# Wider weight chunks for the raw experts: 2048 and 1536 columns in place of 1024, 1024, 1024 and 512

## The chip, the cores and the metric

The kernel runs as one program on one core of a Trainium2 chip (one NeuronCore: TensorE, VectorE, ScalarE, GpSimd, SyncE and 16 DMA engines). The metric is device microseconds (us) of one execution, the median of several runs. A difference of less than 0.2% between two such medians is not told apart here.

## The reference, cut to what matters

Two layers over 256 latent tokens and 256 context tokens of width 1024, all in float32. Layer 0 is a token-mixing MLP and a dense SwiGLU. Layer 1 is windowed attention and a mixture of eight SwiGLU experts, of which each of the 256 latent tokens uses two. The change lies in the experts alone:

```
D_MODEL = 1024; D_FF = 3584; N_EXPERTS = 8; TOP_K = 2
logits = (xt @ w_router).astype(jnp.float32)          # xt: 256 x 1024
top_v, top_i = lax.top_k(logits, TOP_K)
gates = sum(one_hot(top_i) * softmax(top_v))
for e in range(N_EXPERTS):
    y = y + gates[:, e:e + 1] * ((silu(xt @ w_gate[e]) * (xt @ w_up[e])) @ w_down[e])
```

Each expert has three float32 matrices of 3.67 million elements, 44 MB in all; eight experts are 352 MB that are read once.

## The kernel before, in words

Everything ahead of the experts (the first layer, attention, the router) is not touched. The experts begin at about 816 us of the span and last to its end.

**Slots and modes.** The experts are worked off in eight slots, `MODES = "SLSMMSMS"`. Slot 0 is expert 0; the others are given to experts by how many tokens they got. The mode says how many token rows a slot holds: S has 64 rows (one tile of 64), M has 96 rows (three tiles of 32), L has 128. L splits its weights into two halves of fewer bits and multiplies three times; S and M ("raw") feed the float32 weights straight to TensorE as the moving operand, with the tokens as the stationary one. Since an S tile has 64 columns of tokens, two column strips of the array (M: four) work on different columns of the weight row, and their results stand in different partitions of one PSUM bank (`columns`, L1512).

**Chunks and units.** `CH = (1024, 1024, 1024, 512)` cuts the 3584 hidden columns. `expert_units` (L1095) lists the loads in order: for a chunk the gate matrix, then the up matrix, in units of 1 MB, then the down rows of the chunk before. A unit of a 1024-column chunk is 256 weight rows, two in each partition, each a piece of 4 KB in memory; one of the 512-column chunk has four pieces of 2 KB; a unit of down has two whole rows that lie together, 8 KB (in M's last chunk two pieces of 4 KB). An expert is 42 units: 24 + 4 of gate and up, 14 of down.

**Buffers.** Each unit goes into a buffer of 8 KB per partition. After the first 21 the buffers are taken in the fixed order of `CYCLE` (18 names; `yh` and `side1` drop out early, so that 16 are left for the raw experts). All loads are issued by SyncE (SP), in the order of the units; a load waits until the last reader of its buffer is done, and the loads behind it wait too.

**Order on TensorE.** `chunk` (L1692) writes TensorE's order out by hand: gate units of chunk j, up units of chunk j, then the down units of the chunk before. In between stand the transposes of the hidden rows (`transposed_rows`, L1574), and one small step per unit from the list `extras`: the gather of the next expert's tokens (`gather_raw`, L1431: 16 matmuls for each expert), the matrix that brings results back (`back_raw`), and the scatter of an expert's result to token rows (`scattered`, L1625), in which the 64 rows of half a tile are the contraction and both halves use different row strips of the array.

**The end.** After the last down unit come `scaled` (L1615), the last scatter, the final norm and the output.

Of the kernel before, what the change touches and what calls it, by code (L numbers as in the profile page):

```python
# [59 lines left out]
ORDER = ('xgb0', 'xgb1', 'wsx', 'wst5', 'hc', 'wst2', 'wst4', 'yh')  # L60
# [17 lines left out]
MODES = "SLSMMSMS"  # L78
PARTS = {"S": (64, 1), "M": (32, 3)}
# [52 lines left out]
def body(tc, nc, I, out, dbg=None):  # L132
# [9 lines left out]
    with top:  # L142
# [151 lines left out]
        hx = [ph.tile([P, 4, 256], F32, name=f"hx{i}", bufs=1) for i in range(2)]  # L294
# [772 lines left out]
        CH = (1024, 1024, 1024, 512)  # L1067
        ids = {}

        class Expert:  # L1070
# [14 lines left out]
            def long(self, w):  # L1085
                return self.mode != "M" or w == 1024
# [8 lines left out]
        def expert_units(exs):  # L1095
            last = None
            for ex in exs:
                c0 = 0
                for w in CH:
                    k = 2 * 1024 // w  # L1100
                    for which in ("gate", "up"):
                        for r0 in range(0, D, k * P):
                            yield ex, (which, r0, k, c0, w), (k, w)
                    if last is not None:
                        yield from down_units(*last)
                    last = ex, c0, w
                    c0 += w
# [6 lines left out]
        SIZES = {"xgb": 2 * UNIT, "sg": UNIT // 2}  # L1114

        def fill_halves(tiles, src, shape):
            k, n = shape
            return [fill(t, src[:, k // 2 * i:k // 2 * (i + 1)], (k // 2, n)) for i, t in enumerate(tiles)]
# [17 lines left out]
        loaded = [fill_halves([early["sg"], early["at"][:, :UNIT // 2]], *source(first_units[0]))]  # L1136
        loaded += [in_halves(fill(early[n], *source(u))) for n, u in zip(ORDER, first_units[1:])]
# [24 lines left out]
        def stage_load(n, u, behind_):  # L1162
            src, shape = source(u)
            with tc.issue_after(last_early) if behind_ else ExitStack():
                if n == "hx":
                    return fill_halves(early["hx"], src, shape)
                if n in early:
                    return in_halves(fill(early[n], src, shape))
                p = {"wst": wst, "wst3": cur.get("wst3"), "wd": mp}[n]
                return in_halves(fill(p.tile([P, UNIT], F32, name=n, bufs=BUFS[n]), src, shape))  # L1170

        class Halves:
# [5 lines left out]
            def half(self):  # L1178
                if self.raw is None:
                    u = self.units.pop(0)  # L1180
                    self.raw = [moe_load(u), u[2], u[0].mode]
                v, (k, n), mode = self.raw
# [3 lines left out]
                if mode != "L":  # L1186
                    self.ready.append(src)
                    return
# [18 lines left out]
        def raw_row(u, k):  # L1207
            m = u[0].shape[1]
            return u[k // m][:, k % m, :]
# [7 lines left out]
        wrg = con.tile([P, DT, NE], F32, name="wrg")  # L1217
        wrb = con.tile([P, 2, NE], F32, name="wrb")
        ws = s2t()[:, :DT * NE].rearrange("p (k e) -> p k e", k=DT)
        V.tensor_mul(ws, wr, modT[1][:, 24:32, 0:1].to_broadcast([P, DT, NE]))  # L1220
        V.tensor_mul(wrg, wr, G[1][1][:, :, 0:1].to_broadcast([P, DT, NE]))
# [46 lines left out]
        early["hx"] = [ph.tile([P, UNIT // 2], F32, name=f"hx{i}", bufs=1) for i in range(2)]  # L1268
        fills = FILLS.split()
        split_unit = source(units[len(loaded) + [n for n in fills if n != "hx0"].index("hx1")])  # L1270
        parts = []
        for n in fills:
            if n[:2] == "hx":
                src, (k, n_) = split_unit
                i = int(n[2])
                with tc.issue_after(last_early):
                    parts.append(fill(early["hx"][i], src[:, k // 2 * i:k // 2 * (i + 1)], (k // 2, n_)))
                if i:
                    loaded.append(parts)
# [96 lines left out]

        def gather(ex, first=False):
            if ex.mode != "L":
                yield from gather_raw(ex, first)
# [38 lines left out]
        def gather_raw(ex, first):  # L1418
            n = SLOTCAP[ex.col]
            oh = s2t()[:, :2 * n].rearrange("p (c s) -> p c s", c=2)  # L1420
            one_hot(oh, ex, 2, n)
            for _ in range(GY):
                yield
            ex.tile = ph.tile([P, UNIT], F32, name="w", bufs=4)
            ex.xg = ex.tile[:, :DT * n].rearrange("p (d s) -> p d s", d=DT)
            for d0 in range(0, DT, 4):
                ps = tp_ps()
                for d in range(d0, d0 + 4):
# [5 lines left out]
                scaled_rows(ex, ps, d0, 4, n, first)  # L1434
# [3 lines left out]
        def back_raw(ex):  # L1438
# [10 lines left out]
            ex.oht = ex.tile[:, UNIT - 256 * k:].rearrange("p (k t) -> p k t", k=k)  # L1449
# [6 lines left out]
        def scaled_rows(ex, ps, d0, k, n, first):  # L1456
            for d in range(k):
                dst, src, g, b = ex.xg[:, d0 + d, :], ps[:, d * n:(d + 1) * n], G[1][1][:, d0 + d, 0:1], mod(1, 3, d0 + d, 0)
# [52 lines left out]

        def columns(place, xs, wrow, n, start, stop):  # L1512
# [6 lines left out]
        def gate_up(ex, w, steps=()):  # L1519
            per = 2 * 1024 // w  # L1520
# [8 lines left out]
            for k0 in range(0, DT, per):  # L1529
# [15 lines left out]
        def transposed_rows(ex, w):  # L1545
# [7 lines left out]

            if ex.mode == "L":
                at = RB["at"].rearrange("p i (f s) -> p i f s", s=P)
# [9 lines left out]
            nb = w * n // P // P  # L1565
            size = D * n // P
            blocks = [(t, f) for t in range(k) for f in range(nb)]
            at = {}

            def some_blocks(bs):  # L1570
                pt = tp_ps()
                dst = s2t()[:, :len(bs) * P]
                for i, (t, f) in enumerate(bs):
                    PE.transpose(pt[:, i * P:i * P + P], block_of(size * t, f), ident)  # L1574
                    at[t, f] = dst[:, i * P:i * P + P].rearrange("p (h s) -> p h s", s=n)
                A.copy(dst, pt[:, :len(bs) * P])  # L1576

            return [lambda b=b: some_blocks(blocks[b:b + 4]) for b in range(0, len(blocks), 4)], at

        def down(ex, j, w, at):  # L1580
            nf = w // P
            raw = ex.mode != "L"
            if raw:
                n, nt = PARTS[ex.mode]
                nb = nf * n // P
# [207 lines left out]
```

## Time and profile before

| what | value |
|---|---|
| time, median of 3 runs (lowest to highest) | 1680.15 us (1679.33 to 1680.38) |
| the profiled execution's own time | 1678.95 us |
| its span, first to last instruction | 1676.9 us |
| TensorE busy | 1638.3 us, 98% |
| VectorE, ScalarE, GpSimd busy | 47%, 28%, 2% |
| TensorE clock granted, mean | 0.993 |
| bytes moved by the kernel's own queue | 475.73 MB, 75.7% of 16 engines' span |

The profiled execution took 1678.95 us from outside and 1676.9 us from its first to its last instruction, so 2.05 us lie around the span. A matmul of float32 operands shows as two records, so the counts of records are twice those of the program. The ends of matmuls are modelled, so that the duration of a group runs a little into the next; the price of a unit is best read from the start of one group to the start of the next. "Issue" is idle time in which an engine waited for nothing that the profile shows.

### The profile page before, as it was taken

What the parts mean: (1) busy time and instruction counts of PE and PEld (TensorE: products, weight loads), DVE (VectorE), ACT (ScalarE), POOL (GpSimd) and SP (SyncE); (2) the same over time, 40 slices, a digit from 0 to 9 for tenths busy, and PEclk for the clock granted to TensorE, in tenths of its full rate; (3) what the DMA queues carried; (4) which work ended last, traced back from release to release, by engine and by line L of the source; (5) the groups of instructions that cost most, each with busy time, mean ns of one, the idle gap of its engine ahead of it and who ended that gap; (6) DMA issues with size and microseconds to landing.
All of it is one profiled execution on the core that took longest, in us unless ns stands there. A gap on an engine that the chain in (4) does not pass through costs nothing.

```text
span 1676.9 us, 31753 instructions
## 1 busy us (share of the span) xinstructions
PE 1638.3 (98%) x13501; PEld 1122.9 (67%) x13501; DVE 780.9 (47%) x1540; ACT 475.7 (28%) x910; POOL 37.3 (2%) x33
## 2 busy tenths in 40 slices
PE   7999999999999999999999999999999999999997
PEld 4678988888887878888536785355665653556532
DVE  5579678777677856896306984001001001010011
ACT  4434542222222223675215772100000101001001
POOL 0000000000000000032000000000000000000000
PEclk9999999999999999999999999999999999999999
DMA  9865335444455532316999999999999999999994
GB/s 310 284 216 188 125 126 201 151 158 153 142 175 177 191 135 101 101 64 226 392 385 411 412 381 355 408 410 411 407 409 407 383 384 408 409 411 406 405 407 174
DMA packets 178996, 477.83 MB, mean 285 GB/s; under 512 B 9080, under 2 KB 64544, under 8 KB 165152
## 3 DMA queue, kind: packets, MB, share of 16 engines
q1 hardware_dynamic: 178848, 475.73, 75.7%
q8 instruction: 108, 1.77, 0.4%
q14 instruction: 40, 0.33, 0.1%
HBM read 474.65 MB, written 1.05 MB: 284 GB/s over the span
## 4 chain that ended last, share of the span: by engine, by line
PE 93%; DVE 2%; DMA 2%; issue 1%; ACT 1%; SPq 1%; POOL 0%; DVEq 0%; ACTq 0%
PE mm L1516 38%; PE mm L232 15%; PE mm L233 15%; PE mm L234 15%; PE tp L1431 2%; PE tp L1625 1%; PE tp L1574 1%; DMA wst<-in_ada_w_dram 1%; PE mm L1025 1%; DMA side<-in_ctx_dram 1%; PE tp L1010 1%; PE mm L459 1%; PE tp L1446 0%; PE mm L430 0%; DMA side<-in_x_dram 0%
## 5 line engine op out<-in xcount | busy, mean ns | idle before, releaser
L1707 DVE TENSOR_TENSOR sg<-sg,mm 128x512 f32<-128x512 f32 (+2 forms) x47 | 25.6, 569 | 492.3 <-PE mm L1516 489.8
L232 PE MATMUL mm<-b,w 128*128 128x512 f32 (+1 forms) x560 | 206.3, 369 | 0.0
L233 PE MATMUL mm<-b,w 128*128 128x512 f32 (+1 forms) x560 | 205.0, 366 | 0.0
L234 PE MATMUL mm<-b,w 128*128 128x512 f32 (+1 forms) x560 | 204.7, 366 | 0.0
L1516 PE MATMUL mm<-wst,w 128*32 128x256 f32 (+3 forms) x2528 | 195.8, 393 | 4.8 <-issue 4.8
L168 ACT CAST w<-wst 128x512 fp32r<-128x512 f32 (+1 forms) x186 | 112.1, 653 | 170.3 <-PE mm L233 128.4
L496 DVE SCALAR_TENSOR_TENSOR s<-wst,cT,s 128x512 f32<-128x512 f32 x224 | 153.2, 745 | 11.5 <-DMA wst<-in_ada_w_dram 11.5
L1516 PEld LDWEIGHTS mm<-wst,w 128*32 128x32 f32 (+1 forms) x2528 | 96.6, 117 | 90.9 <-issue 53.6
L169 DVE TENSOR_TENSOR w<-wst,w 128x512 fp32r<-128x512 f32 (+1 forms) x186 | 127.1, 725 | 64.2 <-ACT w L168 63.7
L1576 ACT COPY s<-tp 128x512 f32<-128x512 f32 (+2 forms) x37 | 18.6, 503 | 380.8 <-PE tp L1574 321.6
L232 PEld LDWEIGHTS mm<-b,w 128*128 128x128 f32 x560 | 105.6, 189 | 19.6 <-issue 2.5
L234 PEld LDWEIGHTS mm<-b,w 128*128 128x128 f32 x560 | 105.6, 189 | 17.1
L233 PEld LDWEIGHTS mm<-b,w 128*128 128x128 f32 x560 | 105.7, 189 | 16.6 <-DVE b L169 0.2
L1516 PE MATMUL mm<-wst,s 128*32 128x256 f32 (+1 forms) x1104 | 96.3, 417 | 0.1
L232 PE MATMUL mm<-b,side 128*128 128x512 f32 (+1 forms) x240 | 91.0, 379 | 0.0
L234 PE MATMUL mm<-b,side 128*128 128x512 f32 (+1 forms) x240 | 90.0, 375 | 0.0
L233 PE MATMUL mm<-b,side 128*128 128x512 f32 (+1 forms) x240 | 90.0, 375 | 0.0
L1516 PEld LDWEIGHTS mm<-wst,s 128*32 128x32 f32 (+1 forms) x1104 | 44.2, 115 | 47.0 <-issue 27.9
L232 PE MATMUL mm<-w,b 128*128 128x512 f32 (+1 forms) x192 | 73.5, 384 | 0.0
L233 PE MATMUL mm<-w,b 128*128 128x512 f32 (+1 forms) x192 | 72.4, 378 | 0.2 <-DVE w L169 0.2
L234 PE MATMUL mm<-w,b 128*128 128x512 f32 (+1 forms) x192 | 72.1, 376 | 0.0
L1516 PE MATMUL mm<-wd,w 128*32 128x256 f32 (+2 forms) x864 | 70.6, 404 | 0.0
(399 smaller groups left out, 2586.6 us busy)
## 6 DMA issues: line engine op xcount, KB each, us to landing
wst<-in_moe_w_down_dram SPq DMA_DIRECT2D x51, 1024.0 KB, 14.0
wst<-in_moe_w_up_dram SPq DMA_DIRECT2D x50, 1024.0 KB, 15.6
wst<-in_moe_w_gate_dram SPq DMA_DIRECT2D x48, 1024.0 KB, 13.5
wst<-in_ada_w_dram SPq DMA_DIRECT2D x40, 1024.0 KB, 5.2
wd<-in_moe_w_up_dram SPq DMA_DIRECT2D x18, 1024.0 KB, 13.9
xgb<-in_moe_w_gate_dram SPq DMA_DIRECT2D x16, 1024.0 KB, 14.9
wd<-in_moe_w_down_dram SPq DMA_DIRECT2D x16, 1024.0 KB, 14.8
xgb<-in_moe_w_down_dram SPq DMA_DIRECT2D x15, 1024.0 KB, 16.4
```

The lines of the kernel that those rows point to most:

```text
L168: A.copy(hi, src)
L169: V.tensor_sub(lo, src, hi)
L232: PE.matmul(ps, sh, mh, start=start, stop=False)
L233: PE.matmul(ps, sh, ml, start=False, stop=False)
L234: cur["pe"] = PE.matmul(ps, sl, mh, start=False, stop=stop).ins
L459: PE.matmul(ps[j:j + 32, 256 * w:256 * w + 256], ones[:, :32], acc_[s][:, 256 * half_:256 * half_ + 256], start=True, stop=True)
L496: V.scalar_tensor_tensor(acc_[s], u[:, k, :], c_, acc_[s], op0=OP.mult, op1=OP.add)
L1010: PE.transpose(pt[:, kc * P:kc * P + P], pp[b][h4][:, kc * P:kc * P + P], ident)
L1431: PE.matmul(ps[:, (d - d0) * n:(d - d0 + 1) * n], acct[c, h][:, i * P:(i + 1) * P], oh[:, c, :], start=(c == 0), stop=(c == 1))
L1516: PE.matmul(ps[n * g:n * g + n, c0:c0 + w], x, wrow[:, w * g:w * g + w], start=start and first, stop=stop and last)
L1576: A.copy(dst, pt[:, :len(bs) * P])
L1707: V.tensor_mul(x, x, p)
```

## The change

For S and M slots the hidden columns are cut into two chunks, 2048 and 1536; L keeps its four. A unit of gate or up is then one weight row per partition: 8 KB (1 MB in all) in the first chunk, 6 KB (768 KB, in a buffer that could hold 1 MB) in the second. An expert has 46 units: 16 of 1 MB and 16 of 768 KB of gate and up, and 14 of down. The down rows of M's last chunk (now six units) are still pieces of 4 KB.

The rest makes room for it. A chunk of M fills three PSUM banks with 512 (384) columns each, one per tile, and one of S two banks. The hidden rows `sg` and their transposes `at` get one buffer each. The scatter of M works by its 32-row tiles (`scattered`, `quarters`). Two neighbouring slots share one gather (`GROUPED`), 160 token columns wide. The loads that were kept in halves are whole, and the router's scaled weights reuse a tile.

```diff
+GROUPED = (2, 3), (4, 5), (6, 7)
...
-ORDER = ('xgb0', 'xgb1', 'wsx', 'wst5', 'hc', 'wst2', 'wst4', 'yh')
+ORDER = ('at', 'xgb0', 'xgb1', 'wsx', 'wst5', 'hc', 'wst2', 'wst4', 'yh')
...
-        CH = (1024, 1024, 1024, 512)
+        CH = {"L": (1024, 1024, 1024, 512), "S": (2048, 1536), "M": (2048, 1536)}
...
-                return self.mode != "M" or w == 1024
+                return self.mode != "M" or w == 2048
...
-                for w in CH:
-                    k = 2 * 1024 // w
+                for w in CH[ex.mode]:
+                    k = max(2 * 1024 // w, 1)
...
+        def group(ex):
+            for g in GROUPED:
+                if ex.e is None and ex.col in g:
+                    return [order[s] for s in g]
+            return [ex]
...
+        def subs(ex, w):
+            if ex.mode == "S":
+                return [(c, min(1024, w - c)) for c in range(0, w, 1024)]
+            return [(0, w)]
+
+        def pieces(ex, w):
+            n, k = PARTS[ex.mode]
+            return [(t, c, v, v * n // P) for c, v in subs(ex, w) for t in range(k)]
...
-                place, ps = raw_banks(ex, w)
                 n, nt = PARTS[ex.mode]
+                parts = pieces(ex, w)
+                banks = [mm_ps() for _ in parts]
+                ps = [b[:, :hw] for b, (_, _, _, hw) in zip(banks, parts)]
...
-                        columns(place, [ex.xg[:, k, n * t:n * t + n] for t in range(nt)], raw_row(u, k - k0), n, start, stop)
+                        r = raw_row(u, k - k0)
+                        for b, (t, c, v, _) in zip(banks, parts):
+                            columns([(b, 0, True, True)], [ex.xg[:, k, n * t:n * t + n]], r[:, c:c + v], n, start, stop)
...
         def scattered(ps, ex, ys, c):
+            n = PARTS[ex.mode][0]
+            per = 512 * P // (D * n)
             for i, y in enumerate(ys):
-                for h in range(2):
-                    hs = slice(64 * h, 64 * h + 64)
-                    PE.matmul(ps[h], ex.oht[hs, i, c * P:(c + 1) * P], y[hs, :], start=(i == 0), stop=(i == len(ys) - 1))
+                for q in range(P // n):
+                    hs = slice(n * q, n * q + n)
+                    c0 = c % per * y.shape[-1]
+                    PE.matmul(ps[q][:, c0:c0 + y.shape[-1]], ex.oht[hs, i, c * P:(c + 1) * P], y[hs, :],
+                              start=(i == 0 and c0 == 0), stop=(i == len(ys) - 1 and c % per == per - 1))
+
+        def quarters(ex, y):
+            ps = [tp_ps() if q % 2 else mm_ps() for q in range(4)]
+            for c in range(2):
+                scattered(ps, ex, y, c)
+                yield
...
-                    if j == 2 and i + 1 < len(exs):
+                    if j == (2 if ex.mode == "L" else 1) and i + 1 < len(exs) and exs[i + 1] is group(exs[i + 1])[0]:
                         extras.append(gather(exs[i + 1]))
```

**On SP, the loads of slot 0.** The first rows are before, the second after; a name ahead of the arrow is the buffer, and behind the tensor stands the shape in the buffer, partitions first.

```order
L179 DMA yh<-in_moe_w_gate_dram 128x2x1024
L179 DMA wst<-in_moe_w_gate_dram 128x2x1024 x2
L179 DMA hx_7078<-in_moe_w_down_dram 128x1024
L179 DMA wst<-in_moe_w_gate_dram 128x2x1024
L179 DMA wd<-in_moe_w_up_dram 128x2x1024 x3
L179 DMA side<-in_moe_w_up_dram 128x2x1024
L179 DMA w<-in_moe_w_down_dram 128x2048 x2
L179 DMA wst_7096<-in_moe_w_down_dram 128x2048
```

```order
L180 DMA wst_6715<-in_moe_w_gate_dram 128x2048
L180 DMA wst_6713<-in_moe_w_gate_dram 128x2048
L180 DMA wst_6714<-in_moe_w_gate_dram 128x2048
L180 DMA yh<-in_moe_w_up_dram 128x2048
L180 DMA wst<-in_moe_w_up_dram 128x2048 x2
L1123 DMA hx<-in_moe_w_gate_dram 128x768
L180 DMA wst<-in_moe_w_up_dram 128x2048
L180 DMA wd<-in_moe_w_up_dram 128x2048 x3
L180 DMA side<-in_moe_w_up_dram 128x2048
L180 DMA w<-in_moe_w_gate_dram 128x1536 x2
L180 DMA wst_7091<-in_moe_w_gate_dram 128x1536
```

Each load of two rows of 1024 columns has become one row of 2048; the loads that follow are gate rows of 1536 columns, where down rows of the first chunk stood.

**On TensorE, the second half of the last M slot (slot 6).** Before, these are the last gate and up units of its 512-column chunk, with the transposes (L1574) of the chunk before; after, the first gate units of its 1536-column chunk, with transposes (L1605) and the scatter of slot 5 (L1662).

```order
L1574 MATMUL tp<-cst,sg 128x128 x4
L1516 MATMUL mm<-wsx,w 32x128 x48
L1574 MATMUL tp<-cst,sg 128x128 x2
L1516 MATMUL mm<-wst_6716,w 32x128 x48
L1516 MATMUL mm<-hc,w 32x128 x48
L1516 MATMUL mm<-wst_6714,w 32x128 x48
L1516 MATMUL mm<-wst_6715,s_12787 32x256 x8
```

```order
L1605 MATMUL tp<-cst,sg 128x128 x4
L1540 MATMUL mm<-wst,w 32x384 x12
L1605 MATMUL tp<-cst,sg 128x128 x4
L1540 MATMUL mm<-wd,w 32x384 x12
L1605 MATMUL tp<-cst,sg 128x128 x4
L1662 MATMUL tp<-s_11255,w 128x512
L1662 MATMUL mm<-s_11255,w 128x512
L1540 MATMUL mm<-wd,w 32x384 x24
L1662 MATMUL tp<-s_11255,w 128x512
L1662 MATMUL mm<-s_11255,w 128x512
L1540 MATMUL mm<-side,w 32x384 x12
```

A 1 MB unit of the narrow chunk was 48 matmuls of 128 columns; there is no such unit any more, and a 768 KB unit is 12 matmuls of 384 columns.

**On TensorE, the scatter of slot 3 (M) to one half of the tokens.** The first rows are before (three tiles by two halves of 64 rows, 512 columns), the second after (the second and the third tile, each by four quarters of 32 rows, 256 columns; the first tile stands ahead of them in the same way).

```order
L1625 MATMUL tp_10478<-s2_10406,w_8723 128x512
L1625 MATMUL mm_10479<-s2_10406,w_8723 128x512
L1625 MATMUL tp_10478<-s2_10407,w_8723 128x512
L1625 MATMUL mm_10479<-s2_10407,w_8723 128x512
L1625 MATMUL tp_10478<-s2_10408,w_8723 128x512
L1625 MATMUL mm_10479<-s2_10408,w_8723 128x512
```

```order
L1662 MATMUL mm_10044<-s2_9992,w_8105 128x256
L1662 MATMUL tp_10045<-s2_9992,w_8105 128x256
L1662 MATMUL mm_10046<-s2_9992,w_8105 128x256
L1662 MATMUL tp_10047<-s2_9992,w_8105 128x256
L1662 MATMUL mm_10044<-s2_9993,w_8105 128x256
L1662 MATMUL tp_10045<-s2_9993,w_8105 128x256
L1662 MATMUL mm_10046<-s2_9993,w_8105 128x256
L1662 MATMUL tp_10047<-s2_9993,w_8105 128x256
```

Six matmuls of 512 columns into two PSUM banks have become twelve of 256 columns into four.

## Rows read from the trace of the kernel before

**Rows 1.** The page, part 1: busy time, share of span, instructions.

```profile
PE 1638.3 (98%) x13501; PEld 1122.9 (67%) x13501; DVE 780.9 (47%) x1540; ACT 475.7 (28%) x910; POOL 37.3 (2%) x33
```

**Rows 2.** Windows: length, engines' busy time, PE clock, DMA share, GB/s.

```profile
1040.00:1304.00 264.00, 260.36 (x3747) 145.02 (x3747) 26.02 (x59) 21.19 (x51) 0.00 (x0) 0.99 1.02 409
1304.00:1360.00 56.00, 53.90 (x1088) 37.57 (x1079) 1.64 (x4) 4.72 (x13) 0.00 (x0) 1.00 0.97 372
1360.00:1648.00 288.00, 283.89 (x3132) 138.62 (x3130) 29.83 (x67) 21.70 (x49) 0.00 (x0) 0.99 1.02 408
1648.00:1656.00 8.00, 8.00 (x52) 3.59 (x50) 0.42 (x1) 0.00 (x0) 0.00 (x0) 1.00 0.23 93
```

**Rows 3.** Waits of SP's queue, 1304 to 1360 us: sum, times, longest.

```profile
SPq L179 <- PE mm L1516: 40.6, 18, 4.1
```

**Rows 4.** Chain of waits, the end: the first work behind the last down unit.

```profile
1662.29 0.69 DVE s L1615
```

**Rows 5.** Timeline of PE, first unit of slots 3 to 7: start, length.

```profile
1103.39 2.80 PE L1516 MATMUL mm<-wsx,w 128*32 128x256 f32 x48
...
1229.15 2.80 PE L1516 MATMUL mm<-wd,w 128*32 128x256 f32 x48
...
1356.68 7.09 PE L1516 MATMUL mm<-wst,w 128*64 128x512 f32 x32
...
1445.04 5.39 PE L1516 MATMUL mm<-xgb,w 128*32 128x256 f32 x96
...
1571.48 5.37 PE L1516 MATMUL mm<-wd,w 128*64 128x512 f32 x24
```

**Rows 6.** Timeline of PE: the groups behind slot 3's and slot 7's first.

```profile
1106.00 2.77 PE L1516 MATMUL mm<-wst,w 128*32 128x256 f32 x48
...
1576.68 1.89 PE L1516 MATMUL mm<-side,w 128*64 128x512 f32 x8
```

**Rows 7.** DMA view of 1368:1376, 1384:1392 and 1408:1416 us: packets, bytes, rate.

```profile
DMA packets 461, 3.39 MB, mean 424 GB/s; under 512 B 48, under 2 KB 48, under 8 KB 48
...
DMA packets 867, 3.28 MB, mean 410 GB/s; under 512 B 67, under 2 KB 67, under 8 KB 867
...
DMA packets 1565, 3.11 MB, mean 388 GB/s; under 512 B 48, under 2 KB 48, under 8 KB 1565
```

**Rows 8.** Chain of waits around slot 3's narrow chunk: start, length, what.

```profile
1201.28 2.76 PE mm L1516 x96
1204.03 0.44 PE tp L1574 x2
...
1211.53 2.60 issue
```

**Rows 9.** Timeline of PE: narrow chunks' first units (slots 4, 6), and what follows (3, 4, 6).

```profile
1218.22 5.34 PE L1516 MATMUL mm<-wst,s 128*32 128x256 f32 x93
...
1331.94 2.83 PE L1516 MATMUL mm<-wst,w 128*32 128x128 f32 x96
...
1345.62 2.77 PE L1516 MATMUL mm<-wsx,s 128*32 128x256 f32 x47
...
1542.80 2.83 PE L1516 MATMUL mm<-wsx,w 128*32 128x128 f32 x96
...
1560.20 2.02 PE L1516 MATMUL mm<-wst,s 128*32 128x256 f32 x28
```

**Rows 10.** Waits of PE, 1040 to 1662 us: sum, times, longest.

```profile
PE mm L1516 <- issue: 9.8, 6, 2.9
```

**Rows 11.** Timeline of PE: half a gather and half an M scatter, each with its next group.

```profile
1066.97 2.02 PE L1431 MATMUL tp<-s,s 128*128 128x96 f32 x16
1068.92 1.94 PE L1516 MATMUL mm<-xgb,w 128*64 128x512 f32 x8
...
1261.75 0.69 PE L1625 MATMUL tp<-s,w 64*128 64x512 f32 x1
...
1264.53 5.39 PE L1516 MATMUL mm<-wst,w 128*32 128x256 f32 x96
```

More of the change, by code (lines that the diff above doesn't have):

```diff
@@ L292, in body @@
         V.memset(epst, EPS)
-        hx = [ph.tile([P, 4, 256], F32, name=f"hx{i}", bufs=1) for i in range(2)]
+        hxt = ph.tile([P, UNIT], F32, name="hx", bufs=1)
+        hx = [hxt[:, i * UNIT // 2:(i + 1) * UNIT // 2].rearrange("p (d t) -> p d t", d=4) for i in range(2)]
         hc = ph.tile([P, DT, 256], F32, name="hc", bufs=1)
@@ L1112, in down_units, with fill_half @@
                 yield ex, ("down", r0, 2, 0, D, ex.long(w)), (2, D)
-        SIZES = {"xgb": 2 * UNIT, "sg": UNIT // 2}
-        def fill_halves(tiles, src, shape):
+        SIZES = {"xgb": 2 * UNIT, "sg": 1536}
+        def fill_half(t, i, src, shape):
             k, n = shape
-            return [fill(t, src[:, k // 2 * i:k // 2 * (i + 1)], (k // 2, n)) for i, t in enumerate(tiles)]
+            v = view(t, shape)
+            cut = (slice(None), slice(k // 2 * i, k // 2 * (i + 1))) if k > 1 else (
+                slice(None), slice(None), slice(n // 2 * i, n // 2 * (i + 1)))
+            cur["dma"] = nc.sync.dma_start(v[cut], src[cut]).ins
+            return v
         def in_halves(v):
@@ L1207, in raw_row @@
         def raw_row(u, k):
[L1208 to L1209 removed]
+            return u[0][:, k, :]
         def row(u, k):
@@ L1416, in low, with gather_raw @@
             V.tensor_sub(xg[:, 1, d0:d0 + n, :], tmp, xg[:, 0, d0:d0 + n, :])
-        def gather_raw(ex, first):
-            n = SLOTCAP[ex.col]
+        def gather_raw(exs, first=False):
+            ns = [SLOTCAP[ex.col] for ex in exs]
+            n = sum(ns)
+            spans = [slice(sum(ns[:i]), sum(ns[:i + 1])) for i in range(len(ns))]
             oh = s2t()[:, :2 * n].rearrange("p (c s) -> p c s", c=2)
-            one_hot(oh, ex, 2, n)
+            for ex, s in zip(exs, spans):
+                one_hot(oh[:, :, s], ex, 2, SLOTCAP[ex.col])
             for _ in range(GY):
                 yield
-            ex.tile = ph.tile([P, UNIT], F32, name="w", bufs=4)
-            ex.xg = ex.tile[:, :DT * n].rearrange("p (d s) -> p d s", d=DT)
-            for d0 in range(0, DT, 4):
+            t = ph.tile([P, UNIT], F32, name="w", bufs=4)
+            xg = t[:, :DT * n].rearrange("p (d s) -> p d s", d=DT)
+            for ex, s in zip(exs, spans):
+                ex.tile = t
+                ex.xg = xg[:, :, s]
+            per = min(512 // n, 4)
+            for d0 in range(0, DT, per):
                 ps = tp_ps()
-                for d in range(d0, d0 + 4):
+                k = min(per, DT - d0)
+                for d in range(d0, d0 + k):
                     for c in range(2):
@@ L1433, in gather_raw @@
                 yield
-                scaled_rows(ex, ps, d0, 4, n, first)
+                scaled_rows(xg, ps, d0, k, n, first)
             if first:
@@ L1593, in down @@
                     u = unit()
-                start, stop = (j, f) == (0, 0), (j, f) == (len(CH) - 1, nf - 1)
+                start, stop = (j, f) == (0, 0), (j, f) == (len(CH[ex.mode]) - 1, nf - 1)
                 if raw:
-                    columns(ex.place, [at[t, f % nb][:, f // nb, :] for t in range(nt)], raw_row(u, f % 2), n, start, stop)
+                    columns(ex.place, [at[t, f] for t in range(nt)], raw_row(u, f % 2), n, start, stop)
                     continue
@@ L1637, in steps @@
                     yield
+                if ex.mode == "M":
+                    yield from quarters(ex, y)
+                    return
                 for a in range(2):
@@ L1717, in run @@
             for i, ex in enumerate(exs):
-                for j, w in enumerate(CH):
+                for j, w in enumerate(CH[ex.mode]):
                     if j == 1:
```

105 lines of the change are left out of this document (53 added, 52 removed).

## The prediction

> **What bounds the kernel now.** I read the page first: TensorE is busy 98% of the span [rows 1], which by itself says little, since a matmul that waits for nothing and one that waits for weights look much alike there. So I took the windows of the experts' stage next. From 1040 us on the DMA engines are full (share 1.02, 409 and 408 GB/s) except from 1304 to 1360 us, where they move 372 [rows 2]; there SP's queue waits 40.6 us in 18 pieces for TensorE to give buffers back [rows 3]. The last bytes land at about 1648 + 8 x 93 / 408 = 1649.8 us, and TensorE's last down unit is done at 1662.3 [rows 4]. So the loads run ahead, and TensorE ends 12.5 us after them: in the raw experts both are near their limit at once, and the question is which one is late at the end.
>
> The timeline of TensorE answers it. A 1 MB unit of M takes 2.61 us (1103.39 to 1106.00), one of S 1.73 us (1571.48 to 1576.68 for three) [rows 5, 6]. A load takes, from the three stretches with pieces of one size, 2.47 us (8 KB, 424 GB/s), 2.56 us (4 KB, 410) or 2.70 us (2 KB, 388) per 1.0486 MB [rows 7]. A raw expert is then 24 x 2.557 + 4 x 2.703 + 14 x 2.473 = 106.8 us of loading. TensorE spends 125.8, 127.5, 88.4 and 126.4 us on slots 3 to 6 and 90.8 us from slot 7's first unit to the end [rows 5, 4]. So the loads gain some 19 us on TensorE in each M slot and lose 18 in each S slot. Counted back from the 12.5 us of the end, the lead of the loads is 34 us at the start of slot 7, 14 at slot 6, 33 at slot 5, 17 at slot 4 (with the 5.1 us that the loads stood still, 56 x (1 - 372 / 409)) and about 0 at slot 3. At 33 us the buffers were full; at slot 3 TensorE had just caught up.
>
> **What the change does, part by part.**
>
> *TensorE, the narrow chunk.* In M the four units of 512 columns have matmuls of 128 columns, and these take 16.94 us in slot 3 (1201.28 to 1218.22), 13.68 in slot 4 and 17.40 in slot 6 [rows 8, 9], against 4 x 2.61 = 10.4 at the price of the others and 0.4 for transposes. In slot 3 part of the excess stands openly in the chain, as 2.60 us of issue [rows 8]; behind 1040 us TensorE has six such waits, 9.8 us together [rows 10], and by the timeline all six lie in the three narrow chunks. It lacked instructions there, not data. With 512 or 384 columns to a matmul, a quarter to a third of the instructions carry the same bytes, so I take the excess as gone: 6.1 + 2.8 + 6.5 = 15.4 us. Bounds: 0 to 15.4. The wide units I price as the present 256-column ones, 2.61 us per MB (same columns in all).
>
> *TensorE, gathers.* Half a gather takes 1.95 us [rows 11], a whole one 3.9. Those of slots 3, 5 and 7 go: 11.7 us. The two shared ones behind 1040 us have the same number of matmuls as a single one has today; if width counts in full they take 160/96 as long and give back 2 x 2.6 = 5.2. I take nothing, since only their columns grow.
>
> *TensorE, M's scatter.* Half of one takes 2.77 us: six matmuls of 512 columns, in two row strips [rows 11]. Twelve of 256 columns in four strips are 1.4 us if four run side by side, 2.8 if two do, 5.5 if none. I take 1.4, because strips do work side by side in the gate units (24 matmuls of 256 columns in 2.61 us there, 4 of 512 in S in 1.73 [rows 6], so a quarter of the time for half the columns); that is 3 x 2 x 1.4 = 8.2 us saved, at worst 16.4 lost.
>
> TensorE alone would then end at 1662.3 - 15.4 - 11.7 - 8.2 = 1627.0.
>
> *The loads.* A packet of 8 KB takes 309 ns of one engine (16 x 8192 / 424), one of 4 KB 160; halfway, 234.5 for 6 KB, is 419 GB/s and 1.88 us for a 768 KB unit. A raw expert becomes 16 x 2.473 + 16 x 1.876 + 14 x 2.473 = 104.2 us, 2.6 less; M loses 0.3 of that, because six of its down units have 4 KB pieces instead of two. After 1040 us 247 MB were still to come [rows 2], five experts and 26 units of slot 2: 3 x 2.3 + 2 x 2.6 + 1.6 = 13.7 us. No stretch shows 8 KB pieces of gate and up, whose rows do not lie together as those of down do; that they reach 424 is the estimate, bounds 0 and 13.7. With the 5.1 us of standstill gone too, the loads end at 1649.8 - 5.1 - 13.7 = 1631.0.
>
> *Before 1040 us* I count nothing: slots 0 and 1 keep TensorE's work but for one shared gather, and slot 1 (L) is cut as before.
>
> *What is late next.* 1631.0 is behind 1627.0, so at the end TensorE waits for loads. The lead says the same: with 116.2 us for slot 3 (6.1 less, and four S down units at 1.73 in place of M's at 2.61, which come with the slot before), 118.1 for slot 4, 89.2 for slot 5 and 112.5 for slot 6 against 104.2 to 104.6 of loading, it goes 0, 12, 25, 10, 18; slot 7's last 48 units are 98.5 us of TensorE and 119.5 of loading, and it falls below 0. Its peak of 25 is under the 33 at which the loads stood still, but a buffer with 768 KB holds three quarters, and 33 x 0.75 is 25. So a standstill of 0 to 5 us can come back in slot 4; I take 1.5.
>
> *New waits.* M's gate, up and output need eight PSUM banks of six. The up units must wait for ScalarE to empty two gate banks; the matmuls of two other tiles, a third of 2.61 us each, stand between, so I cost it at nothing. If that cover fails, six such places at under 1 us each wait on TensorE, which has 4 us to spare. Scatter and gather steps lie behind them on the same queue, and nobody but TensorE waits for those. SP issues 46 loads per expert in place of 42, each behind the others by design; the count costs nothing while the queue runs ahead.
>
> **The sum.** Loads end 1631.0 + 1.5 = 1632.5. From landing to the first matmul: never seen, as TensorE never waited; 0 to 2, I take 1.0. The last S unit 1.7. TensorE ends at 1635.2. The end behind it is unchanged, 1676.9 - 1662.3 = 14.6: span 1649.8. The profiled execution has 2.05 us around its span, and the median of the runs is 1.2 above it: 1649.8 + 3.25 = 1653.
>
> **The rivals.**
>
> *Longer rows are no faster* (12%). If rows over 4 KB of gate and up load as 4 KB ones do, only the 2 KB pieces gain: 5.6 experts x 0.58 - 3 x 0.34 = 2.2 us. Loads end at 1642.5, and the time is 1642.5 + 1.5 + 1.0 + 1.7 + 14.6 + 3.25 = 1665. For it: gate rows lie 14 KB apart, and no 8 KB piece of such a row was ever timed. Against it: 388, 410, 424 rises with each doubling [rows 7]. [...]
>
> *TensorE keeps its stalls* (8%). If the issue waits come from the supply of instructions and not from short matmuls, 15.4 us stay: TensorE ends at 1642.4, which is after the loads, and the time is 1660. If the scatter's strips don't overlap either, its 8.2 us saved become 16.4 lost, TensorE ends at 1667.0 and the time is 1685, about the old one. For it: issue waits show no releaser. Against it: all six lie where matmuls have 128 columns, none in the wide units, while the loads run alike in both.
>
> *Slower: gate and up rows of 8 and 6 KB load worse* (8%). The place is every gate and up unit of seven slots, as each partition now reads one long piece from rows 14 KB apart, where it read two shorter ones. At 380 GB/s 29.4 MB take 77.3 us against 72.2 today, 28.5 us over 5.6 experts and 1.0 in M's down: loads end at 1674 and the time is 1695. It decides from 393 GB/s down (74.7 us per expert puts the loads' end at 1659.6, and the time at 1680). For it: nothing was measured. Against it: the 2 and 4 KB pieces have the same distance and show only a fixed cost per packet, 9 to 10 ns on top of 75 ns for each 2 KB.
>
> *No change* (6%, of which 1 a small loss): a wait that I don't see, on buffers or banks, eats the gain.
>
> **How the numbers follow.** My forecast has 66%. Its own range is 1648 to 1660 (standstill 0 to 5, landing 0 to 2, a third of the loading term either way). The range for 8 in 10 runs from 1644, a loading term some 9 us better (later experts starting from a fuller queue), to 1668, which takes in the first two rivals. Faster 0.86, the same 0.05, slower 0.09; 0.2% is 3.4 us, about what a measurement of this kernel can tell from no change.
>
> **What would show it.** Right: windows of slots 3 to 7 at some 418 GB/s with a DMA share of 1.02; no issue waits of a us in M; M slots of 112 to 118 us; the last weight bytes near 1632 and TensorE 3 us behind them, waiting for loads in slot 7; half a scatter at 1.4 us. Wrong: gate stretches of 8 KB packets at or below 410 GB/s; standstills of SP on TensorE over 5 us; TensorE ending 10 us after the loads.

## The result, and the profile after

The changed kernel takes **1653.07 us** (median of 4 runs, 1652.86 to 1653.76) against 1680.27 us for the kernel before (1679.33 to 1680.38 in the same job): a ratio of 0.9841, 95% interval 0.9829 to 0.9853, or 27.2 us less. The profiled execution took 1653.76 us with a span of 1651.7 us.

The page, its busy times [rows 1] and the shares of the chain of waits by engine:

```profile
PE 1616.2 (98%) x11173; PEld 1038.8 (63%) x11173; DVE 779.1 (47%) x1533; ACT 469.2 (28%) x877; POOL 37.3 (2%) x33
...
PE 81%; DMA 14%; DVE 2%; ACT 1%; issue 0%; POOL 0%; SPq 0%; DVEq 0%; ACTq 0%
```

The windows of the experts' stage, with the columns of [rows 2]:

```profile
1040.00:1304.00 264.00, 263.91 (x2655) 109.07 (x2655) 28.87 (x61) 20.62 (x40) 0.00 (x0) 1.00 1.02 418
1304.00:1360.00 56.00, 56.00 (x637) 25.75 (x633) 1.90 (x3) 2.63 (x5) 0.00 (x0) 1.00 1.02 415
1360.00:1624.00 264.00, 258.19 (x2378) 106.50 (x2372) 26.88 (x64) 18.66 (x37) 0.00 (x0) 1.00 1.02 418
1624.00:1632.00 8.00, 7.12 (x32) 1.83 (x28) 0.00 (x0) 0.00 (x0) 0.00 (x0) 1.00 0.60 251
```

TensorE is as busy as before (98%), so the page's first line again says little. The chain of waits has 14% DMA now. The loads run at 415 to 418 GB/s where they ran at 372 to 409, and the dip between 1304 and 1360 us is gone: there SP still waits 28.7 us for TensorE, but the DMA share stays 1.02, so those waits don't leave the engines idle:

```profile
SPq L180 <- PE mm L1540: 28.7, 15, 2.8
```

TensorE stands still for 0.1 us from 1040 to 1360 us and for some 6 us from there to 1624 us.

The timeline of TensorE shows where. Its rows are, in order of time: the first units of slots 3 to 7 (1091.45, 1207.31, 1325.13, 1416.19, 1526.70), as in [rows 5]; units of M by which to price them (1104.92, 1283.17); a third of the shared gather (1170.97) and the halves of slot 3's scatter (1271.47, 1275.83), as in [rows 11], with a weight load inside the first half (1272.27, PEld); half of slot 6's scatter (1575.69); and units at the end of slot 7:

```profile
1091.45 2.78 PE L1540 MATMUL mm<-wst,w 128*32 128x512 f32 x24
...
1104.92 2.76 PE L1540 MATMUL mm<-wst,w 128*32 128x512 f32 x24
1107.49 2.76 PE L1540 MATMUL mm<-hx,w 128*32 128x512 f32 x24
...
1170.97 1.90 PE L1446 MATMUL tp<-s,s 128*128 128x160 f32 x12
1172.80 2.14 PE L1540 MATMUL mm<-wd,w 128*32 128x384 f32 x24
...
1207.31 2.78 PE L1540 MATMUL mm<-wst,w 128*32 128x512 f32 x24
...
1271.47 0.48 PE L1662 MATMUL mm<-s,w 32*128 32x256 f32 x1
...
1272.27 0.18 PEld L1662 LDWEIGHTS tp<-s,w 32*128 32x128 f32 x1 [0.49 <-ACT at L1609]
...
1273.76 2.14 PE L1540 MATMUL mm<-hx,w 128*32 128x384 f32 x24
1275.83 0.48 PE L1662 MATMUL mm<-s,w 32*128 32x256 f32 x1
...
1277.34 4.08 PE L1540 MATMUL mm<-xgb,w 128*32 128x384 f32 x48
...
1283.17 2.12 PE L1540 MATMUL mm<-wst,w 128*32 128x384 f32 x24
1285.10 2.12 PE L1540 MATMUL mm<-hc,w 128*32 128x384 f32 x24
...
1325.13 1.94 PE L1540 MATMUL mm<-wst,w 128*64 128x512 f32 x8
...
1416.19 2.78 PE L1540 MATMUL mm<-wst,w 128*32 128x512 f32 x24
...
1526.70 1.94 PE L1540 MATMUL mm<-xgb,w 128*64 128x512 f32 x8
...
1575.69 0.48 PE L1662 MATMUL mm<-s,w 32*128 32x256 f32 x1
...
1577.20 1.51 PE L1540 MATMUL mm<-wst,w 128*64 128x512 f32 x8
...
1602.75 1.94 PE L1540 MATMUL mm<-wst,at 128*64 128x512 f32 x8 [0.37 <-DMA wst<-in_moe_w_down_dram]
1605.23 1.94 PE L1540 MATMUL mm<-wst,at 128*64 128x512 f32 x8 [0.54 <-DMA wst<-in_moe_w_down_dram]
...
1635.06 1.94 PE L1540 MATMUL mm<-hc,at 128*64 128x512 f32 x8 [0.44 <-DMA hc<-in_moe_w_down_dram]
```

Slot 7's units start 2.48 us apart (1602.75 to 1605.23), which is the time of a 1 MB load [rows 7] and not the 1.73 us that TensorE needs for one [rows 6]. From about 1598 us to the end TensorE takes nearly every unit as it lands. Before, TensorE's last units followed the loads by 12.5 us; now it waits for them. VectorE starts on the last unit's output at 1637.04 us (the place of [rows 4]). No wait of a matmul for issue, as in [rows 10], is left between 1040 and 1640 us.

From one group's start to the next group's start is its price: 2.57 us for a 1 MB unit of M, 1.93 for one of 768 KB, 1.83 for a third of the shared gather (two such and a shorter one of 1.29 make 4.95), 2.29 and 1.51 for the halves of slot 3's scatter, 1.51 for half of slot 6's. Inside the 2.29, a weight load stands 0.49 us until ScalarE's copy `at` is done.

The DMA view, windows of 8 us: gate and up pieces of 8 KB (1104:1112), of 6 KB (1152:1160), and M's down pieces of 4 KB (1232:1240), to set beside [rows 7]:

```profile
DMA packets 467, 3.38 MB, mean 423 GB/s; under 512 B 54, under 2 KB 54, under 8 KB 54
...
DMA packets 615, 3.35 MB, mean 419 GB/s; under 512 B 71, under 2 KB 71, under 8 KB 614
...
DMA packets 847, 3.27 MB, mean 409 GB/s; under 512 B 52, under 2 KB 52, under 8 KB 843
```

### The profile page after: what moved, and what is told of

The parts are those of the page before. It is cut to its first block, busy times and chain, and to the rows that moved or that the text cites. A ratio compares the mean times of both kernels' runs of the same rounds, so it can differ in the third digit from the quotient of the medians.

```text
span 1651.7 us, 27054 instructions
## 1 busy us (share of the span) xinstructions
PE 1616.2 (98%) x11173; PEld 1038.8 (63%) x11173; DVE 779.1 (47%) x1533; ACT 469.2 (28%) x877; POOL 37.3 (2%) x33
## 4 chain that ended last, share of the span: by engine, by line
PE 81%; DMA 14%; DVE 2%; ACT 1%; issue 0%; POOL 0%; SPq 0%; DVEq 0%; ACTq 0%
PE mm L1540 27%; PE mm L233 15%; PE mm L234 15%; PE mm L235 15%; DMA xgb<-in_moe_w_up_dram 2%; DMA xgb<-in_moe_w_down_dram 1%; DMA xgb<-in_moe_w_gate_dram 1%; DMA wst<-in_moe_w_up_dram 1%; DMA hc<-in_moe_w_down_dram 1%; DMA wst<-in_moe_w_gate_dram 1%; DMA wd<-in_moe_w_gate_dram 1%; DMA wd<-in_moe_w_down_dram 1%; PE tp L1446 1%; DMA wst<-in_moe_w_down_dram 1%; DMA wst<-in_ada_w_dram 1%; PE mm L1027 1%
## 5 line engine op out<-in xcount | busy, mean ns | idle before, releaser
L1540 PE MATMUL mm<-wst,w 128*32 128x384 f32 (+3 forms) x1464 | 192.5, 541 | 0.4 <-DMA wst<-in_moe_w_up_dram 0.4
L169 ACT CAST w<-wst 128x512 fp32r<-128x512 f32 (+1 forms) x196 | 122.3, 673 | 171.7 <-PE mm L234 125.7
L170 DVE TENSOR_TENSOR w<-wst,w 128x512 fp32r<-128x512 f32 (+1 forms) x196 | 139.4, 752 | 66.7 <-ACT w L169 65.6
L1540 PEld LDWEIGHTS mm<-wst,w 128*32 128x32 f32 (+1 forms) x1464 | 62.7, 118 | 115.9 <-issue 106.8
L1609 ACT COPY at<-tp 128x512 f32<-128x512 f32 (+2 forms) x34 | 18.0, 533 | 400.2 <-PE tp L1605 400.2
L1540 PE MATMUL mm<-wst,at 128*32 128x256 f32 (+1 forms) x1040 | 89.4, 416 | 2.8 <-DMA wst<-in_moe_w_down_dram 2.8
L233 PE MATMUL mm<-b,side 128*128 128x512 f32 (+1 forms) x240 | 91.1, 379 | 0.0
L1540 PE MATMUL mm<-wd,w 128*32 128x384 f32 (+3 forms) x576 | 71.0, 541 | 0.0
L1540 PEld LDWEIGHTS mm<-wst,at 128*32 128x32 f32 (+1 forms) x1040 | 39.8, 114 | 49.4 <-issue 25.2
## 6 DMA issues: line engine op xcount, KB each, us to landing
wst<-in_moe_w_gate_dram SPq DMA_DIRECT2D x34, 1024.0 KB, 19.8
```

The costliest lines, as they stand in the source:

```text
L169: A.copy(hi, src)
L170: V.tensor_sub(lo, src, hi)
L233: PE.matmul(ps, sh, mh, start=start, stop=False)
L1540: PE.matmul(ps[n * g:n * g + n, c0:c0 + w], x, wrow[:, w * g:w * g + w], start=start and first, stop=stop and last)
```

## The experiments

The theory: two streams run side by side from 1040 us on, loads and TensorE, and the later one sets the end; the change sped up both (loads by the length of their rows, TensorE by wider matmuls, shared gathers and a scatter in four strips), and now the loads are the later one. Rival A: the gain is TensorE's. Rival B: the loads' gain hangs on their number or size, not on their rows. In the table, "last unit" is where VectorE starts on the output of the last down unit (the place of [rows 4], 1662.29 before), and the times are medians of 4 runs. The runs come from several jobs, in which the kernel before took 1680.1 to 1680.9 us; each ratio is against the one of its own job.

| kernel | us | ratio to before, 95% interval | against the changed kernel | last unit done |
|---|---|---|---|---|
| before | 1680.27 | | +27.2 | 1662.29 |
| changed | 1653.07 | 0.9841 (0.9829 to 0.9853) | | 1637.04 |
| old pieces | 1670.99 | 0.9942 (0.9925 to 0.9959) | +17.9 | 1654.03 |
| two loads, even and odd | 1659.38 | 0.9871 (0.9855 to 0.9888) | +6.3 | 1642.47 |
| own gathers | 1653.23 | 0.9833 (0.9817 to 0.985) | +0.2 | 1636.26 |
| own gathers, old scatter | 1659.95 | 0.9876 (0.986 to 0.9893) | +6.9 | 1642.50 |
| half of slot 7's down | 1645.08 | 0.9789 (0.9773 to 0.9806) | -8.0 | 1627.36 |
| old pieces, own gathers, old scatter | 1671.1 | 0.9948 (0.9931 to 0.9964) | +18.0 | 1653.98 |
| M in old chunks, 8 KB down rows | 1665.12 | 0.9911 (0.9894 to 0.9928) | +12.0 | 1649.07 |

**Old pieces.** TensorE's work of the changed kernel with the pieces of the one before:

```
 def fill(t, src, shape):
     v = view(t, shape)
+    if shape[0] == 1:
+        h = 1024
+        nc.sync.dma_start(v[:, :, :h], src[:, :, :h])
+        cur["dma"] = nc.sync.dma_start(v[:, :, h:], src[:, :, h:]).ins
+        return v
```

> The changed kernel, with each gate and up load of a raw expert issued as two: 1024 columns and the rest, so rows of 8 KB become 4 + 4 KB and rows of 6 KB 4 + 2 KB, which are the pieces of the kernel before; TensorE's work stays. Theory (the loads end the kernel, and their rate goes with the length of a row): the loads get their 13.7 us back, 1653.1 becomes about 1667, the stretch 1040 to 1304 us goes from 418 to some 409 GB/s, and TensorE waits for loads at more places than slot 7. Rival A (the whole gain was TensorE's: short matmuls, gathers, scatter): 1653, within 1.5. Rival B (the count of loads matters, not the length of their rows): over 1670, with SyncE's queue behind.

1670.99 us, at 407 GB/s (the window stands further down, beside those of two other ways to cut a load), and TensorE idles 4.9 us between 1360 and 1600 us, against 1.0 in the changed kernel. Of the gain 9.9 us are left (1680.87 for the kernel before in that job), though all that TensorE gained is still there: rival A falls. The cost is 4 us above the theory's. In the windows that hold 4 and 2 KB pieces together the rate was 384 to 401 GB/s, in this one (1488 to 1496 us) 393, where the per-packet times of [rows 7] give 402 (16 x 6144 B in 160 + 84.5 ns):

```profile
DMA packets 1143, 3.14 MB, mean 393 GB/s; under 512 B 127, under 2 KB 127, under 8 KB 1142
```

**Two loads with whole rows.** To tell the number of loads from their pieces, each was cut by partitions instead (the same place in `fill`, against the changed kernel):

```
+    if shape[0] == 1:
+        nc.sync.dma_start(v[:64], src[:64])
+        cur["dma"] = nc.sync.dma_start(v[64:], src[64:]).ins
+        return v
```

> The changed kernel, with each gate and up load of a raw expert issued as two again, but cut by partitions (0 to 63 and 64 to 127), so that the rows stay 8 and 6 KB: the count of loads of the run with the old pieces, which took 17.9 us more, without its short pieces. Theory (length of a row): 1653, within 1.5, some 418 GB/s from 1040 to 1304 us. Rival B (the number of loads, or their size): about 1671, some 407 GB/s.

Neither: 2089 us (2048 to 2124), with 248 GB/s at a DMA share of 1.01. The DMA engines are as occupied as in the changed kernel (1.02) and move little more than half of its 418 GB/s. Was it the halves, or the count of loads? The same count was tried with `v[0::2]` and `v[1::2]` in place of `v[:64]` and `v[64:]`.

> The changed kernel, with each gate and up load of a raw expert issued as two, one for the even and one for the odd partitions: full rows of 8 and 6 KB, twice as many loads, and each load spread over all 128 partitions. The run that cut the same loads into partitions 0 to 63 and 64 to 127 moved 248 GB/s and took 2089 us. Theory (length of a row; the halves of the partitions were that run's undoing, not the number of loads): 1653, within 2, some 418 GB/s from 1040 to 1304 us. Rival B (the number of loads, or their size): 1671 or more, 407 GB/s or less, as in the run with the old pieces.

1659.38 us. The windows 1040 to 1304 us of the three, in the order old pieces, halves, even and odd:

```profile
1040.00:1304.00 264.00, 262.02 (x2577) 107.19 (x2577) 32.15 (x61) 23.64 (x44) 0.00 (x0) 1.00 1.03 407
```

```profile
1040.00:1304.00 264.00, 174.70 (x901) 67.35 (x899) 33.64 (x41) 25.96 (x34) 0.00 (x0) 0.92 1.01 248
```

```profile
1040.00:1304.00 264.00, 263.88 (x2611) 108.58 (x2611) 32.15 (x61) 23.71 (x44) 0.00 (x0) 1.00 1.02 416
```

Theory and rival B each have a part: whole rows bring the rate back to 416, but the number of loads is not free, as the theory had it. Of the 17.9 us, 6.3 go with the number (32 more in each of 5.6 raw experts, so some 35 ns each, an estimate) and 11.6 with the length of the rows, for which the theory had 13.7. Without its greater number of loads, the run with the old pieces would have kept some 16 us of the gain, an estimate from 9.9 + 6.3.

**Own gathers; and the old scatter too.** First `GROUPED = ()`, then M's scatter in two row strips of 512 columns besides (the lines of `scaled` and of the extra steps that go with it are left out here):

```
-GROUPED = (2, 3), (4, 5), (6, 7)
+GROUPED = ()
...
-                for q in range(P // n):
-                    hs = slice(n * q, n * q + n)
...
+                for h in range(2):
+                    hs = slice(64 * h, 64 * h + 64)
+                    PE.matmul(ps[h], ex.oht[hs, i, c * P:(c + 1) * P], y[hs, :], start=(i == 0), stop=(i == len(ys) - 1))
```

> The changed kernel with a gather for each slot, as before. TensorE gets three gathers of 3.9 us in place of what the two shared ones take beyond single ones, 9.6 us more behind 1040 us (five of 3.9 against two of 4.95). Theory: TensorE has some 10.5 us to spare, which it waits away in slot 7 (14 units 2.48 us apart with 1.73 us of work each), so the time stays: 1653 to 1655, with the waits of slot 7 nearly gone. Rival A (TensorE ends the kernel): 1662 to 1663.

> As the run with a gather for each slot, and M's scatter in two row strips of 512 columns again (5.5 us a slot against 3.8). TensorE gets 14.8 us in all. Theory: 10.5 of them are covered, 4.3 show: about 1657, the loads standing still again somewhere in the M slots, no waits for loads in slot 7. Rival A: the full sum, 1668. If gathers and scatter don't matter even together: 1653.

1653.23 and 1659.95 us. The last units, first of the kernel with its own gathers, then with the old scatter as well:

```profile
1632.27 1.89 PE L1540 MATMUL mm<-wst,at 128*64 128x512 f32 x8
1634.28 1.94 PE L1540 MATMUL mm<-hc,at 128*64 128x512 f32 x8
```

```profile
1638.85 1.89 PE L1540 MATMUL mm<-wst,at 128*64 128x512 f32 x8
1640.56 1.89 PE L1540 MATMUL mm<-hc,at 128*64 128x512 f32 x8
```

In the first, TensorE has no time left but some 0.3 us ahead of the last unit (2.01 us between two starts, 1.71 without a wait): 9.6 us more of work, none of it in the time. In the second the units follow at 1.71 us without any wait: TensorE ends it. Rival A, which adds both in full, falls. The theory's 1657 was 3 us low; it took TensorE's time to spare as 10.5 us and the added work as 14.8, which the next run measures.

**Half of slot 7's down weights**, which leaves out loads and computes part of the result from the wrong rows:

```
+            k = 1 if ex.col == len(MODES) - 1 and ex.e is None else 2
             for r0 in range(c0, c0 + w, 2 * P):
-                yield ex, ("down", r0, 2, 0, D, ex.long(w)), (2, D)
+                yield ex, ("down", r0, k, 0, D, ex.long(w) and k == 2), (k, D)
...
-            return u[0][:, k, :]
+            return u[0][:, k % u[0].shape[1], :]
```

> The changed kernel, but slot 7 loads only half of the rows of its down weights (128 rows a unit in place of 256) and multiplies them twice, so part of the result is computed from the wrong rows; TensorE's instructions stay, and 7.3 MB, 14 x (2.47 - 1.28) = 16.7 us, of loading are left out at the very end. Theory: TensorE's waits in slot 7 go, some 10.5 us, and TensorE, then alone, ends at about 1626.5: 1642 to 1644. Rival (the end hangs on TensorE, or on the chain behind it): 1653. If TensorE's waits are only in part for data: between.

1645.08 us, 8.0 less. TensorE's last two units:

```profile
1623.71 1.89 PE L1541 MATMUL mm<-wst,at 128*64 128x512 f32 x8
1625.42 1.89 PE L1541 MATMUL mm<-hc,at 128*64 128x512 f32 x8
```

They start 1.71 us apart: TensorE no longer waits at the end, and is done at 1627.36. Two waits for loads are left, ahead of those that were cut:

```profile
1553.81 1.94 PE L1541 MATMUL mm<-xgb,w 128*64 128x512 f32 x8 [0.40 <-DMA xgb<-in_moe_w_up_dram]
...
1556.37 2.80 PE L1541 MATMUL mm<-xgb,at 128*32 128x256 f32 x48 [0.62 <-DMA xgb<-in_moe_w_down_dram]
```

Without their 1.0 us TensorE would be done near 1626.3, an estimate. So its time to spare in the changed kernel is 1637.04 - 1627.36 = 9.7 us by the profiled executions, 8.0 by the medians, and 1.0 more without those waits. Set against the run with own gathers and old scatter, 1642.50 - 1627.36 = 15.1 us, or 16.1 without them, is what gathers and scatter save TensorE (the expectation had 14.8), of which 6.9 show in the time.

**Both setbacks together** (old pieces, own gathers, old scatter).

> The two setbacks together: loads cut into the old pieces (alone 17.9 us more than the changed kernel), a gather for each slot and M's scatter in two strips (alone 6.9 more). Theory (the later of loads and TensorE sets the end): TensorE without waits ends near 1642.5 as in that run, the loads some 12 us later, so the second setback is hidden: 1671, within 2. Rival (the costs add): 1678.

1671.1 us, as with the old pieces alone (1670.99). The two costs, 17.9 and 6.9, do not add: the later stream alone counts.

**Short matmuls.** M's matmuls of 384 columns cut into three, the loads untouched:

```
 w = wrow.shape[-1] * n // P
+s = 128 if w == 384 else w
 for (ps, c0, first, last), x in zip(place, xs):
-    for g in range(P // n):
-        PE.matmul(ps[n * g:n * g + n, c0:c0 + w], x, wrow[:, w * g:w * g + w],
...
+    for b in range(0, w, s):
+        for g in range(P // n):
+            PE.matmul(ps[n * g:n * g + n, c0 + b:c0 + b + s], x, wrow[:, w * g + b:w * g + b + s],
...
```

> The changed kernel, with M's matmuls of 384 columns cut into three of 128, the width of the narrow chunk of before; loads and everything else stay. Theory (short matmuls starve TensorE of instructions): the narrow chunk of before cost 5.1 us more than its columns for 4 MB; 12 MB in each of three M slots cost some 46 us more, 10.5 of it covered: about 1689, with issue waits of a us and more in every second chunk of M, and the loads standing still. Rival C (the stalls come from where the chunk stands, not from the width): 1653. Rival A (TensorE ends the kernel anyway): 1699.

1692.38 us, a ratio of 1.0063 (1.0045 to 1.0081): slower than before. Waits of TensorE from 1040 us, and its timeline in slot 3's second chunk:

```profile
PE mm L1542 <- issue: 30.9, 21, 3.3
```

```profile
1158.96 2.17 PE L1542 MATMUL mm<-wst,w 128*32 128x128 f32 x72
1160.95 0.61 PE L1542 MATMUL mm<-hc,w 128*32 128x128 f32 x15
1162.88 1.80 PE L1542 MATMUL mm<-hc,w 128*32 128x128 f32 x57 [1.31 <-issue]
```

With the same data and place the issue waits of [rows 10] are back, 21 in place of six, and rival C falls. But the rows say more than the theory did: a unit of 72 short records that meets no wait takes 1.99 us (1158.96 to 1160.95), hardly more than the 1.93 of the wide one. Short matmuls are not slow in themselves; TensorE stands still between them for 0.3 to 3.3 us at a time. The view names no releaser, but the DMA view has a queue that brings instructions, in packets of 16 KB; from 1150 to 1200 us, in this run and in the changed kernel:

```profile
q8 instruction: 8, 0.13, 1.1%
```

```profile
q8 instruction: 5, 0.08, 0.7%
```

By the trace's record of single packets, each of the 21 waits ends 1.3 to 1.6 us after such a packet has landed, and so do the six of [rows 10] and the thirteen of the two runs with M in old chunks below (1.2 to 1.5 us). From 1148 to 1217 us the packets land 5.9 to 6.4 us apart, whether TensorE stands or not. So it most likely waits for its next instructions, which short matmuls use up faster than they come. That these packets are TensorE's own, and what sets their pace, is not shown.

**Old chunks for one mode.** `CH` of S or of M set back to `(1024, 1024, 1024, 512)`.

> The changed kernel with S in chunks of 1024, 1024, 1024, 512 columns again, M in 2048 and 1536. Theory: S's matmuls are as wide as M's were in the wide chunks, so TensorE loses nothing; the loads lose 2.6 us in slots 5 and 7 and 1.6 in what is left of slot 2: about 1660. Rival A (only M's short matmuls counted): 1653 to 1655.

> The changed kernel with M in chunks of 1024, 1024, 1024, 512 columns again, S in 2048 and 1536. Theory: the loads lose 2.3 us in each M slot, 6.9; TensorE gets the 15.4 us of the narrow chunks back, 10.5 of them covered, 4.9 over. The later of the two sets the end: about 1660, issue waits in the narrow chunks again. Rival A (TensorE ends the kernel): 1653 + 15.4 = 1668. Rival D (rows and width don't matter, only gathers and scatter): 1653.

S: 1663.42 us, 10.3 more where the theory had 7. In the profiled execution 8.0 of it lie ahead of the last unit (1645.03 against 1637.04); the end behind that took 16.4 us in place of 14.7, and why was not traced. The loads' rate explains most of the 8.0: 413 GB/s from 1360 to 1600 us (417 in the changed kernel), and 381 from 1600 to 1624 us (421), where SP waits for a buffer that TensorE has not given back:

```profile
SPq L180 <- PE mm L1540: 8.4, 2, 6.5
```

M: 1664.83 us where the theory had 1660. The edit had also turned all of M's down rows to pieces of 4 KB, which was mended in another run (`long` for chunks of 1024 columns):

> M in chunks of 1024, 1024, 1024, 512 columns again, now with the down rows of its wide chunks in pieces of 8 KB as in the kernel before (the run before this one had 4 KB in all 14 units, 8 units a slot x 0.084 = 2.0 us more in three slots, beside its 11.8). Theory: 2 us less than that run, 1663, with issue waits in the narrow chunks as before. Rival (TensorE's narrow chunks end this kernel, loads don't): 1665 unchanged.

1665.12 us: no gain, and here the rival was right. TensorE has these waits from 1040 us on:

```profile
PE mm L1540 <- issue: 11.3, 7, 2.5
...
PE mm L1540 <- DMA wst<-in_moe_w_down_dram: 1.1, 2, 0.6
```

Slot 7's last units follow without a wait, so TensorE ends this kernel, at 1649.07: M's old chunks cost it 21.7 us over the 1627.36 of the run with half the down weights, not 15.4. Some 11 us stand as issue waits, and behind two of them the granted clock was 0.50 (1339.50 to 1342.00 us) and 0.55 (1547.30 to 1550.00); how the rest divides among more transposes, the third PSUM bank and waits early in slot 3 was not traced.

## Why the prediction was right, point by point

- **Which stream ends the kernel.** Right, and shown four ways: slot 7's units come at the pace of the loads; with less to load the end moves forward 8.0 us; with 9.6 us more for TensorE it doesn't move; two setbacks cost no more than the larger. The M slots were put at 116.2, 118.1 and 112.5 us and took 115.9, 117.8 and 110.5 (the differences of the starts above); slot 5 took 91.1 against 89.2.
- **TensorE alone** was to end at 1627.0 and does at 1627.4, or 1626.3 without the 1.0 us of waits, but two terms were mis-sized against each other. Gathers and scatter were put at 19.9 us and save 15.1 to 16.1: a shared gather costs 4.95 us and not 3.9, for as many records (32), of 160 columns in place of 96, and the scatters of M cost 3.8, 3.0 and 3.0 and not 2.8 (by these prices 9.6 + 6.8 = 16.4). Only slot 3's first half takes 2.29 us where every other takes 1.51, and 0.5 of that is the wait for ScalarE at 1272.27. The chunks were put at 15.4 and save the rest, 1662.3 - 1642.5 = 19.8. The wide units gained too, 2.57 us against the 2.61 assumed.
- **The narrow chunks' excess** of 15.4 us was right to be taken as gone, and the trace of the kernel before shows more of it than the six waits (9.8 us). Behind the two longest, 2.6 and 2.9 us, the granted clock fell to 0.50 and 0.51 (the windows below), for some 3.4 us each; 81 records then took 4.15 us where 78 had taken 2.38, so that the two stretches cost some 3.4 us together, an estimate; in the changed kernel the granted clock is 1.00 from 1040 to 1640 us. The prediction set supply of instructions and short matmuls against each other as rivals; by the run with short matmuls they belong together.

```profile
1214.80:1217.80 3.00, 3.00 (x64) 2.98 (x60) 0.00 (x0) 0.00 (x0) 0.00 (x0) 0.50 1.05 415
1556.00:1559.50 3.50, 3.50 (x76) 3.50 (x71) 0.00 (x0) 0.00 (x0) 0.00 (x0) 0.51 1.04 412
```

- **The loads.** 8 KB rows of gate and up run at 423 GB/s (424 assumed), 6 KB rows at 419 (the estimate halfway), so the slower rival, with its 393 GB/s, falls. The rival of longer rows that are no faster falls too: whole rows of 8 and 6 KB moved 416 GB/s, and rows cut to 4 and 2 KB 407 with the same number of loads. The term of 13.7 us has the right size: the rows alone measure 11.6, rows and number together 17.9. Four more loads per expert were counted as free; at 35 ns they are some 0.8 us (4 x 5.6 x 35 ns, an estimate).
- **New waits.** None that counts: TensorE's matmuls wait for ScalarE once behind 1040 us, 0.5 us in slot 7, where the kernel before has the same wait; the one weight load in slot 3's scatter is the other.
- **The standstill of 1.5 us in slot 4** did not come: SP does wait for TensorE, 28.7 us of it between 1304 and 1360 us, but the DMA share stays 1.02. Beside it the prediction counts slot 7's last units as 48; they are 52, its own 46 and six down units of slot 6, and the 98.5 and 119.5 us are right for 52.
- **The end.** That it came out right to 0.1 us is luck: errors of opposite sign cancel. Reckoned as the prediction did, the loads end at 1624 + 8 x (251 + 30) / 418 = 1629.4 us (30 GB/s is the rate from 1632 to 1640 us), 3.1 sooner than 1632.5. Of that 1.5 is the standstill; another 1.5, an estimate, was gained before 1040 us, where the prediction counted nothing. From there on the kernel's own queue moved 246.96 MB before and 246.34 after, 0.6 MB less:

```profile
q1 hardware_dynamic: 61601, 246.96, 93.9%
```

```profile
q1 hardware_dynamic: 39930, 246.34, 90.6%
```

  But the last unit began at 1635.06, 5.7 us behind that and not 1.0: the last loads did not stop at once, but thinned out (251 GB/s from 1624 to 1632 us), as those of before had done (254, 205 and 213 GB/s in the three microseconds from 1648 us on). It took 2.0 us (1.7 assumed), the end behind it 14.66 us (14.6 assumed), so the span is 1651.7 and not 1649.8. Against that, 3.25 us were added for what lies around the span and for the median; it was 1.4 (1653.07 - 1651.7).

## What to carry to other kernels

When two streams share a stage, a share of busy time for either says little (TensorE's was 98% in both kernels here); price one unit of each, follow who leads from stage to stage, and ask which is late at the last one. A change that speeds up both is worth what the later one then allows: here TensorE's gain without the longer rows gave 9.9 us of 27.2 (some 16, by the estimate above, with no more loads than the changed kernel has), and more than half of the 15 to 16 us that gathers and scatter saved lay in time that TensorE would have waited anyway. Then test it with two setbacks at once: if their costs add, the theory of a later stream is wrong.

## What had not been expected of the hardware

- **Partitions and rate.** Loads of 64 neighbouring partitions moved 248 GB/s from 1040 to 1304 us at a DMA share of 1.01 (with the down units, which were not cut, among them), and 232 to 236 in three windows of cut 6 KB rows (1120 to 1168 us); the same loads cut into even and odd partitions moved 416. The two halves stood in the queue one behind the other and did not bring the rate back. What sets the lower rate is not shown.
- **A load more cost some 35 ns**, an estimate from 6.3 us over some 180 loads, with rows unchanged and the DMA engines full (share 1.02 from 1040 to 1304 us); only cuts into even and odd partitions were tried.
- **Short matmuls** of 128 columns cost hardly more per byte (1.99 us against 1.93 for a unit of 768 KB) until TensorE stands, 0.3 to 3.3 us at a time; in all four traces that have such waits, 40 in all, each ends 1.2 to 1.6 us after a packet of instructions has landed.
- **Two waits cost twice.** Behind the issue waits of 2.6 and 2.9 us of the kernel before, the granted clock was 0.50 for over 3 us. It was not so behind each: with M in old chunks it stayed 1.00 behind one of 2.5 us (1214.50 to 1217.50 us).
